# Both MLP products of a decoder block as seven block products each, with the inner layer stored in DRAM as operand pairs

## The chip, the cores and the metric

The kernel runs on one core of a Trainium2 chip. Its time is the device time of one launch, in microseconds (us); the kernel before takes 2312.52 us, the median of 3 runs (2311.11 to 2315.71). Engines: TensorE (PE; its weight loads are PEld), VectorE (DVE), ScalarE (ACT), GpSimd (POOL) and SyncE (SP), which here only issues DMAs. SBUF is the memory that all engines read; TensorE writes to the eight banks of PSUM.

## The reference

One decoder layer over 1024 tokens of width 1024, in float32. The part that the change touches is its end, the MLP:

```python
x = x + merged @ w_o                                  # "Wo": 1024 x 1024
h2 = rms_norm(x, norm_mlp_g)
x = x + jnp.square(jax.nn.relu(h2 @ w_mlp_in)) @ w_mlp_out   # 1024 x 4096, then 4096 x 1024
```

Ahead of it stand a projection, differential attention, a short convolution, attention over a memory and a gated merge of the three. They are the same in both kernels.

## The kernel before

All matrix products work on pairs: a float32 operand is kept as hi (a float32r rounding) and lo = raw - hi, and one product is three passes, hi*hi + hi*lo + lo*hi. A pair costs one ACT copy with rounding (L196 for weights) and one subtraction, on DVE or POOL by turns (L178).

Wo (L840 to L862) goes over three column groups of w_o (384, 384 and 256 wide) and, in each, over eight tiles of 128 tokens. In the last group `x2_norm` (L824) norms a finished token tile into `xn`, and `h2.put` (L233) transposes it on TensorE and splits it; the first four tiles are put between the passes of later Wo tiles (L848 to L851), the other four between the passes of the first MLP columns (L884 to L887).

The MLP goes over the hidden layer in 16 groups of 256 columns. `up` (L865) makes 128 hidden columns for 512 tokens in 24 matmuls of 512 columns, then relu (ACT, L876), square (POOL, L877), and the split into uh and ul (ACT L878, DVE L879). The second product takes the group's 256 rows of w_mlp_out for all 8 token tiles and both 512-column halves, 6 matmuls each, and DVE adds the two PSUM banks of a tile to `acc` in SBUF (L908, 1024 wide). In the last group each half is added and stored at once (L914).

Each product of the MLP is so 1536 matmuls of 512 columns: 3072 in all.

TensorE runs its instructions in the order of the program (`T.pin`, L80), loads on SP likewise (L92). The order on DVE, ACT and POOL is set by a scheduler. Each engine works through its own queue in order and waits for semaphores.

Of the kernel before, what the change touches and what calls it, by code (L numbers as in the profile page):

```python
# [15 lines left out]
F32 = mybir.dt.float32  # L16
# [8 lines left out]
P = 128  # L25
# [30 lines left out]
def tile_hybrid_block(ctx: ExitStack, tc: tile.TileContext, x, mem, norm_mix_g, norm_mem_g, w_in, b_gate,  # L56
# [9 lines left out]
    class InOrder:  # L66
        """Instructions of one queue, kept in the order of the program."""
# [10 lines left out]
    class T:  # L78
        """The tensor engine."""
# [26 lines left out]
    pool = ctx.enter_context(tc.tile_pool(name="pool", bufs=1))  # L106
    psum = ctx.enter_context(tc.tile_pool(name="psum", bufs=2, space=PSUM))
# [72 lines left out]
    def load_w(src, n, kind, eng=None):  # L180
        """src [K, n] -> (his, los), over k tiles, of [128, n] float32r APs."""
# [21 lines left out]
    def mm3_steps(ps, lhs, rhs):  # L203
        """ps = sum over k of lhs[k]^T rhs[k]; lhs, rhs = (his, los). Yields after each pass."""
# [10 lines left out]
    class ByTok:  # L215
        """[1024 channels, 1024 tokens] pair written by token tiles: slots of 2 k tiles and 512 tokens."""
# [16 lines left out]
        def put(self, t, xn, parts=(0, 4)):  # L233
            """Transposes the rows xn [128 tok, 1024] into place."""
# [11 lines left out]
    class ByChan:  # L246
        """The same written by channel tiles: a slot for each k tile."""
# [15 lines left out]
    def norm_rows(xt, g_row, step=D):  # L263
        """rms-normed rows [128, 1024] times the gain, in place."""
# [18 lines left out]
    # ================= memory: keys and values =================  # L283
# [30 lines left out]
    def normed(ps):  # L314
        """ps [128, 256] rms-normed along its rows, in SBUF."""
# [26 lines left out]
    def put_x(t):  # L342
        """The next half of a token tile."""
# [44 lines left out]
    # ================= memory attention =================  # L388
# [3 lines left out]
    def q_proj(i):  # L392
        """Yields after each pass; the last leaves the normed rows."""
# [7 lines left out]
    def run(gen, n=None):  # L401
        """Advances gen by n steps (all of them without n)."""
# [53 lines left out]
    # ================= filler work beside the attention: convolution, gate logits =================  # L456
# [39 lines left out]
    def fill_steps():  # L496
# [5 lines left out]
        # the last two units by halves, so that the first half of hT is free early  # L502
# [13 lines left out]
    # ================= output projections of the branches, gated merge =================  # L516
# [6 lines left out]
    def prep(b):  # L523
        """Loads of a branch: first weights, the branch's rows."""
# [56 lines left out]
    # ================= differential attention =================  # L581
# [19 lines left out]
    def qkv(s):  # L601
        """Projections of token tile t for head h, norms of q and k."""
# [24 lines left out]
    def qk_transposes(s):  # L627
# [7 lines left out]
        # q of either component on both halves of the partitions; k's hi, and on the other half what it leaves  # L635
# [14 lines left out]
    def scores(s):  # L650
        """Scores, softmax numerators; e0 becomes e0 - e1 * lam * s0 / s1."""
# [13 lines left out]
        for c in range(2):  # L665
            sc = scs[c]
            # sc = -(sc + mask), negm = -max(sc + mask)
# [30 lines left out]
    def values(s):  # L698
        """o = a v / s0, rms-normed along the head's 128 columns."""
# [88 lines left out]
    for s in range(ns):  # L788
        # steps of the filler: before the scores, beside the softmax, before the values, behind them
# [28 lines left out]
    # ================= output projection, residual =================  # L818
    acc = [slot(f"acc{t}", F32) for t in range(NT)]
    h2 = ByTok("h2")  # L820
# [3 lines left out]
    def x2_norm(t):  # L824
# [3 lines left out]
        xn = xns[t] = rowt("xn")  # L828
        V.scalar_tensor_tensor(out=xn, in0=acc[t], scalar=r, in1=g2_row, op0=ALU.mult, op1=ALU.mult)

    us = {}
    w1 = {}
    NB = DFF // 256

    def load_w1(j):
        if j < 2 * NB:
            w1[j] = load_w(w_mlp_in[:, j * P:(j + 1) * P], P, "wh")

    w = ready.pop("wo")
    for j, (c0, n, _) in enumerate(wos):  # L840
        for t in range(NT):
# [5 lines left out]
            steps = mm3_steps(ps, mT.tok(t), w)  # L847
            if j == 2 and 2 <= t < 6:  # L848
                for k0 in (0, 4):
                    run(steps, 10)  # L850
                    h2.put(t - 2, xns[t - 2], (k0,))  # L851
            run(steps)
# [3 lines left out]
            if j == 2:  # L856
                if t == 0:
                    h2.alloc(0)
                if t == 6:
                    load_w1(0)  # L860
                x2_norm(t)
        w = wn  # L862

    # ================= MLP =================
    def up(j, hf):  # L865
        run(up_steps(j, hf))

    def up_steps(j, hf):
        """relu(h2 @ w1)^2 for 128 columns of the hidden layer, half of the tokens."""
        if hf == 0:  # L870
            us[j] = [slot(f"u{c}") for c in "hl"]
        sl = slice(hf * 512, (hf + 1) * 512)
        ps = ps_mm()
        yield from mm3_steps(ps, w1[j], h2.half(hf))
        r = small("osl", (P, 512))
        A.activation(r, ps, AF.Relu)  # L876
        G.tensor_tensor(out=r, in0=r, in1=r, op=ALU.mult)  # L877
        A.copy(out=us[j][0][:, sl], in_=r)  # L878
        V.tensor_tensor(out=us[j][1][:, sl], in0=r, in1=f(us[j][0])[:, sl], op=ALU.subtract)  # L879

    load_w1(1)
    h2.alloc(1, "m")
    steps = chain(up_steps(0, 0), up_steps(1, 0))
    for t in range(4, NT):  # L884
        for k0 in (0, 4):
            run(steps, 6)
            h2.put(t, xns[t], (k0,))  # L887
    run(steps)
    up(0, 1)
    load_w1(2)  # L890
    w2 = load_w(w_mlp_out[0:256, :], S, "fw")
# [56 lines left out]
```

## Time and profile before

| | us |
|---|---|
| median of the runs | 2312.52 |
| span of the profiled execution | 2311.5 |
| Wo, first to last matmul | 1511.4 to 1604.5 |
| MLP, last matmul ends | 2308.2 |
| PE busy over the span | 2273.5 (98%) |
| DVE, ACT, POOL busy | 1105.3, 889.2, 645.0 |

Shares of busy time are means over very different stages. In the MLP TensorE is never idle, while DVE is busy for 231.5 of 600 us and POOL for 126.4 (the stretch from 1650 to 2250 us).

### The profile page before, as it was taken

The numbers are of one execution on the slowest core, as the hardware profiler recorded it, in microseconds if no ns is written. First come the engines' busy times: TensorE is split into PE (matmuls) and PEld (weight loads), VectorE is DVE, ScalarE is ACT, GpSimd is POOL, SyncE is SP. The second block draws the span as 40 slices with busy tenths as digits, with TensorE's granted clock in tenths as the row PEclk, the third lists the DMA queues.
The fourth block names the chain that finished last, engine by engine and source line by source line (L and its number), as shares of the span: only waits on it lengthen the run. The fifth ranks groups of instructions, "written<-read, shape, count | busy, mean of one in ns | idle before, by whom it ended". The sixth has DMA issues, their size and how long they took to land.

```text
span 2311.5 us, 31433 instructions
## 1 busy us (share of the span) xinstructions
PE 2273.5 (98%) x11814; PEld 1974.5 (85%) x11814; DVE 1105.3 (48%) x2164; ACT 889.2 (38%) x2244; POOL 645.0 (28%) x837
## 2 busy tenths in 40 slices
PE   6999999999999999999999999999999999999999
PEld 6999888888888888888887888899888888888887
DVE  6655455555555555555556234325334434434334
ACT  5644454454545454544446233323221221221220
POOL 4422223232323232232324133312221221221211
PEclk9999999999999999999999999999999999999999
DMA  6312111121212121221214444323111111111111
GB/s 196 128 64 65 46 62 58 48 80 48 71 42 83 42 80 31 69 60 40 80 51 151 137 134 158 120 80 94 54 46 46 55 46 46 55 46 46 53 30 73
DMA packets 185992, 168.39 MB, mean 73 GB/s; under 512 B 14064, under 2 KB 163824, under 8 KB 185840
## 3 DMA queue, kind: packets, MB, share of 16 engines
q1 hardware_dynamic: 166512, 136.86, 19.1%
q10 hardware_dynamic: 19328, 29.52, 3.6%
q8 instruction: 93, 1.52, 0.3%
q14 instruction: 59, 0.48, 0.1%
HBM read 137.00 MB, written 29.36 MB: 72 GB/s over the span
## 4 chain that ended last, share of the span: by engine, by line
PE 91%; DVE 3%; ACT 2%; DMA 2%; issue 1%; POOL 0%; SPq 0%; ACTq 0%; DVEq 0%; POOLq 0%
PE ps_mm L84 60%; PE ps_sc L84 26%; PE ps_tr L88 3%; PE ps_tr L84 3%; DVE ql L646 1%; ACT qh L641 1%; DMA rawh<-in_w_in_dram 1%; ACT whi L196 0%; DMA raw<-in_w_mem_kv_dram 0%; DMA memt<-in_mem_dram 0%; POOL wlo L178 0%; DVE e L680 0%; DVE whl L178 0%; DVE wlo L178 0%; DMA raw<-in_w_in_dram 0%
## 5 line engine op out<-in xcount | busy, mean ns | idle before, releaser
L84 PE MATMUL ps_mm<-hT,whi 128*128 128x512 f32 x1536 | 491.0, 401 | 0.9 <-DVE vst L616 0.9
L178 POOL TENSOR_TENSOR wlo<-raw,whi 128x384 fp32r<-128x384 f32 (+3 forms) x192 | 233.7, 1220 | 648.4 <-ACT whi L196 645.1
L196 ACT CAST whi<-raw 128x256 fp32r<-128x256 f32 (+3 forms) x392 | 206.7, 561 | 458.2 <-PE ps_sc L84 309.7
L84 PEld LDWEIGHTS ps_mm<-hT,whi 128*128 128x128 f32 x1536 | 279.4, 189 | 52.5 <-DVE vst L616 3.9
L84 PE MATMUL ps_mm<-h,whi 128*128 128x512 f32 x1024 | 316.0, 390 | 0.0
L84 PE MATMUL ps_mm<-hT,wlo 128*128 128x512 f32 x768 | 302.2, 394 | 0.0
L84 PE MATMUL ps_mm<-whh,hT 128*128 128x384 f32 x1024 | 276.4, 340 | 1.9 <-DVE inner L465 1.9
L178 DVE TENSOR_TENSOR wlo<-raw,whi 128x256 fp32r<-128x256 f32 (+2 forms) x200 | 172.1, 863 | 162.2 <-ACT whi L196 161.4
L908 DVE TENSOR_TENSOR acc<-ps_sc,acc 128x1024 f32<-128x1024 f32 x120 | 147.0, 1225 | 197.9 <-PE ps_sc L84 197.9
L84 PEld LDWEIGHTS ps_mm<-h,whi 128*128 128x128 f32 x1024 | 191.6, 188 | 39.2
L84 PE MATMUL ps_mm<-h,wlo 128*128 128x512 f32 x512 | 199.3, 389 | 0.0
L84 PE MATMUL ps_sc<-wlo,uh 128*128 128x512 f32 x496 | 192.7, 389 | 0.0
L84 PE MATMUL ps_sc<-whi,ul 128*128 128x512 f32 x496 | 192.7, 389 | 0.0
L84 PE MATMUL ps_sc<-whi,uh 128*128 128x512 f32 x496 | 192.7, 389 | 0.0
L84 PEld LDWEIGHTS ps_mm<-whh,hT 128*128 128x128 f32 x1024 | 186.3, 188 | 7.2 <-DVE inner L465 3.7
L84 PE MATMUL ps_mm<-whl,hT 128*128 128x384 f32 x512 | 171.4, 335 | 0.0
L84 PEld LDWEIGHTS ps_mm<-hT,wlo 128*128 128x128 f32 x768 | 144.7, 188 | 27.5
L618 POOL TENSOR_TENSOR sq<-qk 128x256 f32<-128x256 f32 x64 | 43.2, 675 | 392.1 <-ACT qk L613 391.8
L168 POOL TENSOR_TENSOR r<-r,mhalf 128x1 f32<-128x1 f32 (+1 forms) x186 | 132.0, 710 | 15.3
L167 POOL TENSOR_SCALAR r<-ss 128x1 f32<-128x1 f32 (+1 forms) x186 | 36.9, 198 | 321.8 <-ACT ps_tr L712 127.7
L84 PE MATMUL ps_mm<-x,whi 128*128 128x512 f32 x384 | 118.9, 391 | 0.0
L84 PE MATMUL ps_sc<-x,whi 128*128 128x512 f32 x384 | 118.3, 389 | 0.0
(176 smaller groups left out, 4083.0 us busy)
## 6 DMA issues: line engine op xcount, KB each, us to landing
raw<-in_w_in_dram SPq DMA_DIRECT2D x56, 512.0 KB, 3.8
raw<-in_w_mlp_in_dram SPq DMA_DIRECT2D x32, 512.0 KB, 4.1
raw<-in_w_mlp_out_dram SPq DMA_DIRECT2D x32, 512.0 KB, 3.7
rawh<-in_w_in_dram SPq DMA_DIRECT2D x64, 192.0 KB, 2.8
z_dram<-z ACTq DMA_DIRECT2D x24, 512.0 KB, 3.0
gt<-z_dram SPq DMA_DIRECT2D x24, 512.0 KB, 3.7
raw<-in_w_mem_kv_dram SPq DMA_DIRECT2D x16, 512.0 KB, 5.8
xt<-in_x_dram SPq DMA_DIRECT2D x8, 512.0 KB, 4.1
```

What stands on the lines that cost most here:

```text
L84: return cls.pin(nc.tensor.matmul(*a, **kw))
L88: return cls.pin(nc.tensor.transpose(*a, **kw))
L167: G.tensor_scalar(r, ss, 1.0 / n, EPS, op0=ALU.mult, op1=ALU.add)
L168: G.tensor_tensor(out=r, in0=r, in1=mhalf[:, 0:width], op=ALU.pow)
L178: eng.tensor_tensor(out=lo, in0=raw, in1=f(hi), op=ALU.subtract)
L196: A.copy(out=hi[:, a:b, :], in_=raw[:, k0 + a:k0 + b, :])
L618: G.tensor_tensor(out=sq, in0=qk, in1=qk, op=ALU.mult)
L641: A.activation(qh[z, c, :], tp[a, 0, :], AF.Copy, scale=gcol[a, :])
L646: V.scalar_tensor_tensor(out=ql[z, c, :], in0=tp[a, 0, :], scalar=gcol[a, :], in1=f(qh)[a, c, :], op0=ALU.mult, op1=ALU.subtract)
L908: V.tensor_tensor(out=acc[t], in0=ps, in1=acc[t], op=ALU.add)
```

## The change

Both MLP products are cut into 2x2 blocks, and the four blocks of the result are made from seven block products in place of eight. The operands of the seven are sums and differences of blocks: with a for the blocks of the weights, s1 = a21 + a22, s2 = s1 - a11, a11 - a21 and a12 - s2, and the same forms for the other operand (t1 to t4). The sum is made in float32, and each operand is then split into a pair. `ORDER` names the seven.

- **Wo** is left as it is, but `xn` of each token tile and the residual `acc` go to DRAM (`xn_dram` on ACT's queue, `x2_dram` on SP's queue), and all pools are closed behind it.
- **X operands**: `x_pair` loads two token tiles, transposes them, and makes the seven pairs X for these tokens, 256 of the 1024 tokens at a time (128 of each half): 9 ACT instructions, 8 on DVE and 3 on POOL.
- **First product**: 16 units of 2x128 hidden columns; a unit is seven products of 12 matmuls (K = 512, 512 columns). `Weights.make` makes the seven weight pairs of a unit, up to 5 products ahead. Unit 0 is run twice, with 256 columns each, the second time for the tokens of the last two `x_pair`s. Three partial sums of a unit stay in PSUM and are copied by ACT (`snap`) while later products go on adding to the same bank. The four results are made on DVE (`out`), their three differences and t4 on POOL and DVE by turns (`later`), and all seven are split (`emit`) and stored to `u_dram`, 512 KB each, on SP's queue.
- **Second product**: 8 chunks of 512 hidden rows; a chunk is seven products of 4 token tiles, each 6 matmuls of 512 columns. Its operands come back from `u_dram`, 1 MB each, four products ahead; the seven pairs of w_mlp_out are made three products ahead. After each product DVE adds each PSUM bank to `acc2` (512 wide). The residual is added from `x2_dram` by POOL in chunks 2 and 3.

The core of the diff:

```diff
+        store(xn_dram[t], xn)
+        nc.sync.dma_start(x2_dram[t], acc[t])
...
+    old.close()
+    ORDER = (1, 2, 6, 5, 7, 4, 3)
+    def split(hi, lo, raw, eng):
+        A.copy(out=hi, in_=raw)
+        sub(eng, lo, raw, f(hi))
...
+            if i == 6:
+                self.s1, self.s2 = self.temp(), self.temp()
+                add(self.sums(), self.s1, a21, a22)
+                sub(self.sums(), self.s2, self.s1, a11)
+                raw = self.s2
...
+            hi, lo = self.op[i] = self.pair()
+            split(hi, lo, raw, self.los())
...
+    usums, ulos, tsums = Turns([V]), Turns([G, V, G]), Turns([G, V])
...
+            if src is None:
+                A.activation(t, ps, AF.Relu)
+                V.tensor_tensor(out=t, in0=t, in1=t, op=ALU.mult)
+            else:
+                add(V, t, ps, src)
+                V.scalar_tensor_tensor(out=t, in0=t, scalar=0.0, in1=t, op0=ALU.max, op1=ALU.mult)
...
+            split(hl[:, 0, :], hl[:, 1, :], raw, ulos())
+            nc.sync.dma_start(u_dram[u // 2, k - 1, :, :, u % 2, cs], f(hl))
...
+        load_unit1(0)
+        rows = {p: row_blocks(p) for p in range(2)}
...
+        ahead = 5
+        for n in range(ahead):
+            prep1(seq, n)
+        x_pair(0, rows[0])
+        rows[2] = row_blocks(2)
+        x_pair(1, rows[1])
...
+        for n, (u, i, c0, cn) in enumerate(seq):
+            prep1(seq, n + ahead)
...
+            product1(u, i, c0, cn)
+            run_later(1)
...
+    dsums, dlos = Turns([V]), Turns([G, G, V, G, G, V, G])
...
+        load_u(seq2, n + 4)
+        prep2(seq2, n + 3)
...
+            mm7(ps, [[uo[:, h, k, p * P:(p + 1) * P] for k in range(2)] for h in range(2)],
+                [[wt[h][:, k, :] for k in range(2)] for h in range(2)], i in (1, 2, 5))
...
+            if c == 0 and i in (1, 6, 5, 4):
+                A.copy(out=a, in_=ps)
+            else:
+                add(V, a, ps, a)
```

V is DVE, G is POOL, A is ACT; `Turns([G, V, G])` hands the calls to the engines in that rotation. `mm7` issues the three passes for each K tile.

The first place is DVE at the end of Wo. Before: `xn` is the normed tile, `h2` its transposed pair, `wlo` a weight's lo part.

```order
L829 SCALAR_TENSOR_TENSOR xn_16431<-acc6_15550,r_16428,g_row_15553 128x1024
L854 TENSOR_TENSOR acc7_15551<-ps_mm_16435,qd_16433 128x256
L178 TENSOR_TENSOR wlo_16476<-raw_16469,whi_16475 128x384
L178 TENSOR_TENSOR wlo_16660<-raw_16657,whi_16659 128x384
L826 TENSOR_REDUCE ss_16462<-sums2_15552 128x1
L244 TENSOR_TENSOR h2110_16487<-ps_tr_16500,h2010_16483 128x2x128
```

In the changed kernel `w1` is a weight's pair and `st` one of its sums, `w1raw` the loaded block, `tp` a transposed tile in PSUM, `x11` the lo part of X1:

```order
L836 SCALAR_TENSOR_TENSOR xn_16389<-acc7_15553,r_16386,g_row_15555 128x1024
L877 TENSOR_TENSOR w1_16441<-w1raw_16416,w1_16441 128x512
L880 TENSOR_TENSOR st_16444<-w1raw_16416 128x512
L877 TENSOR_TENSOR st_16445<-st_16444,w1raw_16416 128x512
L877 TENSOR_TENSOR st_16454<-w1raw_16416 128x512
L877 TENSOR_TENSOR st_16585<-w1raw_16416,st_16445 128x512
L877 TENSOR_TENSOR x11_16403<-tp_16459,x10_16402 128x4x128
```

The weights' and the tokens' preparation that stood between Wo's tiles now stands behind the last of them, in one piece.

The second place is POOL in the middle of the MLP. Before, in one group of the hidden layer (`osl` is the squared relu):

```order
L877 TENSOR_TENSOR osl_19714<-osl_19714 128x512
L178 TENSOR_TENSOR wlo_19832<-raw_19825,whi_19831 128x384
L877 TENSOR_TENSOR osl_19744<-osl_19744 128x512
L877 TENSOR_TENSOR osl_19790<-osl_19790 128x512
L178 TENSOR_TENSOR wlo_20028<-raw_20025,whi_20027 128x384
L178 TENSOR_TENSOR wlo_20036<-raw_20025,whi_20035 128x256
```

Now, in the first product, `hl` is a split result on its way to `u_dram`, `t1` and `t2` are differences of results (`b`):

```order
L877 TENSOR_TENSOR hl_17490<-b11_17487,hl_17490 128x512
L877 TENSOR_TENSOR t1_17512<-b12_17509,b11_17314 128x512
L877 TENSOR_TENSOR t2_17559<-b22_17413,t1_17512 128x512
L877 TENSOR_TENSOR w1_17569<-st_17566,w1_17569 128x512
L877 TENSOR_TENSOR hl_17537<-t3_17535,hl_17537 128x512
L877 TENSOR_TENSOR hl_17561<-t2_17559,hl_17561 128x512
```

And DVE in the same unit (`Z` is a PSUM bank, `u2` and `u3` are ACT's copies of one):

```order
L880 TENSOR_TENSOR b12_17509<-Z_17373,u2_17360 128x512
L877 TENSOR_TENSOR w1_17543<-st_17541,w1_17543 128x512
L1053 SCALAR_TENSOR_TENSOR b12_17509<-b12_17509 128x512
L877 TENSOR_TENSOR st_17714<-w1raw_17295,st_17566 128x512
L877 TENSOR_TENSOR t3_17535<-b22_17413,b12_17509 128x512
L877 TENSOR_TENSOR hl_17514<-t1_17512,hl_17514 128x512
```

Every POOL row, and every DVE row but the first, has both inputs in SBUF.

## Rows read from the trace of the kernel before

**Rows 1.** The page: busy us of the engines, TensorE's granted clock by slices.

```profile
PE 2273.5 (98%) x11814; PEld 1974.5 (85%) x11814; DVE 1105.3 (48%) x2164; ACT 889.2 (38%) x2244; POOL 645.0 (28%) x837
PEclk9999999999999999999999999999999999999999
```

**Rows 2.** Chain of waits from Wo to the end: start us, us, what.

```profile
1511.39 73.54 PE ps_mm L84 x442
1584.93 0.44 PE ps_tr L88 x4
1585.36 1.19 PE ps_mm L84 x10
...
1598.23 6.25 PE ps_mm L84 x52
...
1644.41 21.76 PE ps_sc L84 x96
...
2307.44 0.73 PE ps_mm L84 x6
...
2308.20 0.42 DVE acc L914
```

**Rows 3.** Stretches: busy us of PE, PEld, DVE, ACT, POOL, PE clock, DMA share, GB/s.

```profile
0.00:30.00 30.00, 15.92 (x100) 15.15 (x101) 15.45 (x26) 15.90 (x37) 13.36 (x29) 1.00 0.87 241
39.40:42.80 3.40, 3.40 (x18) 3.40 (x19) 1.15 (x3) 1.12 (x4) 0.74 (x2) 0.54 0.35 95
1650.00:2250.00 600.00, 600.00 (x2649) 496.99 (x2648) 231.54 (x218) 126.77 (x215) 126.40 (x108) 1.00 0.15 47
```

**Rows 4.** Instructions of single tiles: count, ns shortest/median/longest.

```profile
L571 POOL TENSOR_TENSOR merged<-merged,gt x32: 1278/1293/1675, 1347.3 to 1512.2; 128x512 f32<-128x512 f32 x32
L879 DVE TENSOR_TENSOR ul<-osl,uh x64: 681/692/1091, 1617.3 to 2289.7; 128x512 fp32r<-128x512 f32 x64
L914 DVE TENSOR_TENSOR acc<-ps_mm,acc x9: 425/691/692, 2287.7 to 2308.2; 128x512 f32<-128x512 f32 x8, 128x256 f32<-128x256 f32 x1
L908 DVE TENSOR_TENSOR acc<-ps_sc,acc x120: 1224/1225/1225, 1647.2 to 2275.5; 128x1024 f32<-128x1024 f32 x120
```

**Rows 5.** Timeline from 1242 us, POOL, then DVE: start us, us, instruction.

```profile
1247.46 3.57 POOL L178 TENSOR_TENSOR x<-rawx,x 128x512 fp32r<-128x512 f32 x2 [1.63 <-ACT x L538]
1248.07 3.50 DVE L178 TENSOR_TENSOR x<-rawx,x 128x512 fp32r<-128x512 f32 x2
```

**Rows 6.** Groups by form: busy us, mean ns of one, idle before.

```profile
L196 ACT CAST whi<-raw 128x512 fp32r<-128x512 f32 x120 | 68.6, 620 | 30.4 <-PE ps_mm L84 12.7 <-issue 10.7 <-DMA raw<-in_w_mem_kv_dram 4.8
...
L178 POOL TENSOR_TENSOR wlo<-raw,whi 128x512 fp32r<-128x512 f32 x60 | 82.2, 1370 | 105.6 <-ACT whi L196 105.4
...
L178 POOL TENSOR_TENSOR wlo<-raw,whi 128x1024 fp32r<-128x1024 f32 x16 | 40.5, 2532 | 301.3 <-ACT whi L196 301.3
...
L178 DVE TENSOR_TENSOR wlo<-raw,whi 128x1024 fp32r<-128x1024 f32 x16 | 39.4, 2460 | 0.5 <-ACT whi L196 0.5
```

**Rows 7.** The page: DMA queues (MB, share of 16 engines), issues (us to landing).

```profile
q1 hardware_dynamic: 166512, 136.86, 19.1%
q10 hardware_dynamic: 19328, 29.52, 3.6%
...
raw<-in_w_mlp_in_dram SPq DMA_DIRECT2D x32, 512.0 KB, 4.1
...
z_dram<-z ACTq DMA_DIRECT2D x24, 512.0 KB, 3.0
```

**Rows 8.** PE before that clock drop: start us, us, [idle before <-releaser].

```profile
36.96 0.39 PE L84 MATMUL ps_sc<-wlo,memTh 128*128 128x256 f32 x1 [2.11 <-DVE wlo L178]
39.22 0.39 PE L84 MATMUL ps_sc<-wlo,memTh 128*128 128x256 f32 x1 [1.64 <-POOL wlo L178]
40.76 0.41 PE L84 MATMUL ps_sc<-whi,memTl 128*128 128x256 f32 x1
40.97 0.41 PE L84 MATMUL ps_sc<-whi,memTh 128*128 128x256 f32 x1
```

More of the change, by code (lines that the diff above doesn't have):

```diff
@@ L816, in tile_hybrid_block @@
     run(stream)
+    x2_dram = dram.tile([NT, P, S], F32, name="x2_dram")
+    xn_dram = dram.tile([NT, P, S], F32, name="xn_dram")
     acc = [slot(f"acc{t}", F32) for t in range(NT)]
-    h2 = ByTok("h2")
     sums2 = const.tile([P, NT, 3], F32, name="sums2")
@@ L846, in tile_hybrid_block @@
             ps = ps_mm(n)
[L847 to L852, printed above, removed]
+            mm3(ps, mT.tok(t), w)
             a = acc[t][:, c0:c0 + n]
@@ L856, in tile_hybrid_block @@
             if j == 2:
[L857 to L860, printed above, removed]
                 x2_norm(t)
         w = wn
[L865 to L879, printed above, removed]
@@ new lines, in mm7 @@
+    def mm7(ps, lhs, rhs, start):
+        n = len(lhs[0])
+        for k in range(n):
+            for i, (a, b) in enumerate(((0, 0), (0, 1), (1, 0))):
+                T.matmul(ps, lhsT=lhs[a][k], rhs=rhs[b][k], start=start and k == 0 and i == 0,
+                         stop=k == n - 1 and i == 2, skip_group_check=True)
+    xp = ctx.enter_context(tc.tile_pool(name="xp", bufs=1, reuse_waits="tile"))
+    bp = ctx.enter_context(tc.tile_pool(name="bp", bufs=1, space=PSUM, reuse_waits="tile"))
@@ new lines, in bank, with slot8, raw8, half_row @@
+    def bank(name):
+        return bp.tile([P, 512], F32, tag="b", bufs=8, name=name)
+    def slot8(name, shape, dtype=F32R):
+        return xp.tile([P, *shape], dtype, tag="x", bufs=14, name=name)
+    def raw8(name):
+        return xp.tile([P, 2048], F32, tag="wraw", bufs=2, name=name)
+    X = {i: [slot8(f"x{i}{c}", (4, 512)) for c in range(2)] for i in ORDER}
+    def half_row(name):
+        return xp.tile([P, 512], F32, tag="stg", bufs=8, name=name)
+    def row_blocks(p):
+        rows = {}
+        for t in range(2):
+            for kh in range(2):
+                rows[kh, t] = half_row("xr")
+                load(rows[kh, t], xn_dram[2 * p + t][:, kh * 512:(kh + 1) * 512])
+        return rows
@@ new lines, in x_pair, with tps, put @@
+    def x_pair(p, rows):
+        cols = slice(p * P, (p + 1) * P)
+        def tps(kh, th):
+            tp = bank("tp")
+            for j in range(4):
+                T.transpose(tp[:, j * P:(j + 1) * P], rows[kh, th][:, j * P:(j + 1) * P], ident)
+            return tp
+        def put(i, src, eng):
+            hi, lo = (X[i][c][:, :, cols] for c in range(2))
+            split(hi, lo, src.rearrange("p (k n) -> p k n", k=4), eng)
+        b11 = tps(0, 0)
+        put(1, b11, V)
+        r11 = half_row("r11")
+        A.copy(out=r11, in_=b11)
+        b12 = tps(0, 1)
+        t1 = half_row("t1")
+        sub(V, t1, b12, r11)
+        r12 = half_row("r12")
+        A.copy(out=r12, in_=b12)
+        put(5, t1, G)
+        b22 = tps(1, 1)
+        t2 = half_row("t2")
+        sub(V, t2, b22, t1)
+        put(6, t2, G)
+        t3 = half_row("t3")
+        sub(V, t3, b22, r12)
+        put(7, t3, G)
+        put(3, b22, V)
+        b21 = tps(1, 0)
+        put(2, b21, V)
+        t4 = half_row("t4")
+        sub(V, t4, b21, t2)
+        put(4, t4, V)
@@ new lines, in tile_hybrid_block, with load2, begin2, temp @@
+    body()
+    w2v = w_mlp_out.rearrange("(c g u p) n -> p c g u n", c=NC, g=2, u=2, p=P)
+    dsums, dlos = Turns([V]), Turns([G, G, V, G, G, V, G])
+    W2, raw2, U = {}, {}, {}
+    def load2(c):
+        raw2[c] = [raw8("w2raw").rearrange("p (u n) -> p u n", u=2) for _ in range(2)]
+        for g in range(2):
+            load(raw2[c][g], w2v[:, c, g])
+    def begin2(c):
+        r = raw2.pop(c)
+        a11, a12, a21, a22 = (r[g][:, :, n0:n0 + 512] for n0 in (0, 512) for g in range(2))
+        def temp():
+            return xp.tile([P, 2, 512], F32, tag="hl", bufs=6, name="st2")
+        def pair():
+            t = slot8("w2", (2, 2, 512))
+            return t[:, 0], t[:, 1]
+        W2[c] = Weights(a11, a12, a21, a22, temp, pair, dsums, dlos)
@@ new lines, in prep2, with load_u @@
+    def prep2(seq, n):
+        if n < len(seq):
+            c, i = seq[n]
+            if i == 1:
+                begin2(c)
+            W2[c].make(i)
+            if i == 3 and c + 1 < NC:
+                load2(c + 1)
+    def load_u(seq, n):
+        if n < len(seq):
+            c, i = seq[n]
+            t = U[c, i] = slot8("uop", (2, 2, 512))
+            (store if n < 4 else load)(f(t), u_dram[c, i - 1])
+    seq2 = [(c, i) for c in range(NC) for i in ORDER]
+    acc2 = []
+    with tc.high_priority(offset=300):
+        load2(0)
+        for n in range(3):
+            prep2(seq2, n)
+            load_u(seq2, n)
+            if n == 1:
+                for p in range(NP):
+                    pair = slot8(f"acc{p}", (2, S), F32)
+                    acc2 += [pair[:, 0], pair[:, 1]]
```

187 lines of the change are left out of this document (141 added, 46 removed).

## The prediction, made before the changed kernel had run

> **What bounds the kernel now.** First the busy line and the clock line of the page [rows 1]: TensorE is busy 98% of the span, and its clock is full in all forty slices, so before the change a matmul less is time less. Second the chain of waits [rows 2]. From 1511.4 us to the last matmul it is TensorE all the way: 96 matmuls of 512 columns take 21.76 us, 0.2267 each, ten of 256 columns 1.19 us, 0.119 each. 3072 x 0.2267 = 696.3 us is the MLP. From Wo's last matmul (1598.23 + 6.25 = 1604.5) to the last one (2308.2) are 703.7 us, which leaves 7.4: 3.5 for eight groups of transposes of 0.44 and 3.9 lost. Third the stretch from 1650 to 2250 us [rows 3]: TensorE 600 of 600, DVE 231.5, POOL 126.4. Here the other engines have room, and the change spends it.
>
> **What is removed.** The first product becomes 15 units of 84 matmuls of 512 columns, and one run as 168 of 256; the second is 8 chunks of 168 of 512. (1260 + 1344) x 0.2267 + 168 x 0.119 = 610.3 us against 696.3: 86.0 saved. A unit is 19.0 us of TensorE, a chunk 38.1. The rest is what this uncovers.
>
> **Prices.** POOL takes 1.29 us for a two-input operation of 512 columns, DVE 0.69, from SBUF or with one input in PSUM [rows 4]. But both have a long side, 1675 and 1091 ns, and where both engines work on SBUF without a pause [rows 5] two on POOL take 3.57 us and two on DVE, at the same time, 3.50. So a pair costs about 1.75 us; one after the other they would take 1.98, side by side 1.29. A DVE operation with PSUM input is never slowed: 1224 to 1225 ns over 120 [rows 4]. ACT's cast of 512 takes 0.62 [rows 6]. I take 1.75 for each pair of a POOL and a two-SBUF-input DVE operation, bounds 1.29 and 1.98.
>
> The Trainium skill (page "SBUF — State Buffer", section "Who interferes with whom") calls the port pair that the two share an exclusive lock, held for whole instructions. The trace agrees in direction: both stretch. By the lock a pair would cost the full 1.98; the row has 1.75.
>
> **Start-up of the first product.** Before, weights and tokens are prepared between Wo's tiles. Now this stands behind Wo's last tile. Without the transposes Wo ends at 1604.5 - 3.5 = 1601.0. Behind it, on SP's queue, come the last residual's store, two weight loads of 512 KB and the row loads. A store of 512 KB takes 3.0 us to land, a load 4.1 [rows 7]; norm, store and reload in series put the first work on tokens at about +9. From there to the last X operand DVE has 28 operations of 512 with PSUM input (19.3 us), 14 with two SBUF inputs (9.7) and 8 of 256 columns, 0.425 each [rows 4], 3.4: together 32.4, plus about 6 behind POOL's 17 operations (half of them meeting, 0.7 each). 1601 + 9 + 32.4 + 6 = about 1649 for X and with it the start of the main stage. Bounds: 1640 (no collision, loads early) and 1664 (every collision and a late store). TensorE has only 27 us of work in these 48, so it waits in pieces of microseconds. The clock answers to that: after waits of 2.11 and 1.64 us [rows 8] it stood at 0.54 from 39.4 to 42.8 us [rows 3], with 256-column matmuls 0.21 us apart in place of 0.12. If all 27 us ran so, they would be 27 x 0.21 / 0.119 = 48, the same as DVE's time; so I cost the clock at nothing here.
>
> **First product.** From 1649 to the last weight pair of the first product POOL has 157 operations of 512, 13 of 256 and one of 1024, as 165.5 of 512; DVE 204 of 512 and 11 of 256 with two SBUF inputs, as 209.5, and 41 of 512 from PSUM. TensorE has 15 units, 285.6 us. Each engine alone fits under that: POOL 165.5 x 1.29 = 213.5, DVE 209.5 x 0.69 + 42.5 x 0.69 = 174, ACT 265 x 0.62 = 164. Together on the port: 165.5 pairs x 1.75 = 289.6, and the other 44 of DVE x 0.69 = 30.4, which makes 320 us, 34 over TensorE. DVE's PSUM operations go beside POOL's own work, and weight pairs are made up to five products ahead, so most waits are absorbed; I add 6 for what is not, 326 (21.7 a unit). Bounds: 285.6 (TensorE) and 213.5 + 144.6 = 358 (every operation at its full duration, none beside another).
>
> Cost at nothing: the stores of results and the loads of weights, 4.72 MB a unit. The queues moved 136.86 MB in 19.1% of the span, 310 GB/s when at work [rows 7], by which a unit needs 15.2 us, under 21.7. The first 30 us had 241 GB/s at 0.87 share [rows 3]; at 241 it is 19.6 us. ACT's snaps run under the products that follow, as long as the bank's next use is a product later.
>
> **From the first to the second product.** TensorE's last unit ends 2.7 us behind its last weight pair (one product, 12 x 0.2267). Then the second product needs its own weights, prepared in the posts' way on the same two engines (21 DVE operations stand behind the first product's last weight pair), and operands that are stored and loaded back: 3.0 + 4.1 us in series [rows 7]. The first chunk's operands were stored long before; the last units' belong to chunk 8 alone. I take 8 us, between 3 and 12.
>
> **Second product.** 1344 x 0.2267 = 304.7. In a chunk of 38.1 us DVE has 28 adds of one bank (0.69 each, 19.3) and 6 operations of 1024 with two SBUF inputs, between 1.22 (the bank form [rows 4]) and 2.46 (beside POOL [rows 6]), so 26.6 to 34.1; POOL 5 of 2.53, 12.7, and 8 residual adds in two of the chunks (10.3 more). DVE is close but under. Loads are 9.4 MB a chunk, 30 us at 310 GB/s, 39 at 241: close too. I take 6 us of stalls, between 2 and 10. The end is as before, with an add of 512 in place of 256: before 2311.5 - 2308.2 = 3.3 us, now 3.3 + 0.27, taken as 3.8 for the wider store.
>
> **Sum.** 1649 + 326 + 2.7 + 8 + 304.7 + 6 + 3.8 = 2300.2 us of span. The median lies 1.0 above the profiled execution's 2311.5, so 2301 us.
>
> **Rivals.**
> (B) Collisions are hidden and TensorE bounds the first product. For it: each engine alone fits with 70 us to spare, and the shortest cases (1278 and 681 ns) show pairs that miss each other. Against it: [rows 5]. X at 1649, unit 0's last product about 3 us behind it: 1652 + 285.6 + 3 + 304.7 + 2 + 3.8 + 1.0 = 2252.
> (C) Slower: POOL's and DVE's operations exclude each other in full in the first product, and TensorE waits for weight pairs in every unit. Price 358 us in place of 326; it decides over faster or slower once this stage passes 337 us, 22.5 a unit (2301 + 11 = 2312). 1649 + 358 + 2.7 + 12 + 304.7 + 10 + 3.8 + 1.0 = 2341. For it: every POOL row of the first product reads two tiles in SBUF, and the waits are short and many, which is what dropped the clock in [rows 8]. Against it: 1.75, not 1.98, where the two met without pause. The lock rule of the Trainium skill, named above, would end here.
> (D) DMA bounds the first product. If stores and loads mixed on one queue fall to 196 GB/s, as an estimate a fifth under the 241 of [rows 3], a unit takes 24.1 us: 1649 + 361 + 2.7 + 12 + 304.7 + 10 + 3.8 + 1.0 = 2344. Against it: 310 GB/s [rows 7].
> That the change doesn't do what it says I rule out: the program holds 2772 matmuls in place of 3072.
>
> **How the numbers follow.** The forecast (the port binds part of the time) 0.60, with a range of its own from 2278 (main stage 310, transition and stalls at their low ends) to 2325 (X at 1655, main stage 340, the rest a little over); B 0.16; C 0.18; D 0.06. A measurement of this kernel tells no change from 0.2%, 2307.9 to 2317.1 us. Of the forecast's 0.60, 0.41 is below that, 0.11 in it and 0.08 above. Faster 0.41 + 0.16 = 0.57, same 0.11, slower 0.08 + 0.18 + 0.06 = 0.32. The range takes in most of B and of C: 2256 to 2340.
>
> **What the profile after would show.** A unit of the first product 21 to 22.5 us apart, not 19.0; POOL's operation of 512 at a mean of 1.5 or more and DVE's with two SBUF inputs above 0.85, against 1.29 and 0.69; TensorE's waits there released by the weight pairs' lo parts on POOL or DVE; 20 to 25 us of idle TensorE between 1601 and 1652; a chunk of the second product within 1.5 us of 38.1. Wrong would be: units at 19.1 (B); units at 24 with waits on the stores' buffers or on weight loads (D); or means at the low end with TensorE waiting all the same, in which case the order of the queues binds and not the port. If TensorE's clock stands well under 1.0 in the first product, waits cost twice and C is nearer.

## The result, and the profile after

The changed kernel takes 2341.4 us, the median of 4 runs (2341.14 to 2342.15), against 2314.11 for the kernel before on the same chip: 1.0119 times as long, 95% interval 1.0105 to 1.0133. It is slower, by 1.2%; the forecast was 2301 and faster, and the time lies 1.4 us above the range.

First the page of the changed kernel (busy us, then tenths in 40 slices and the granted clock), to be held against [rows 1]:

```profile
PE 2219.3 (95%) x11508; PEld 1920.4 (82%) x11508; DVE 1369.4 (59%) x2449; ACT 975.6 (42%) x2363; POOL 917.2 (39%) x965
...
PE   6999999999999999999999999996899898799999
...
DVE  5755455555555555555555324316788888566665
...
POOL 4422232232322232323224133303687778445322
PEclk9999999999999999999999999998999999899999
```

TensorE is busy for 54 us less than before and yet the span is 28 longer. In the first product (the 29th to the 34th slice) DVE is at 7 to 8 tenths and POOL at 6 to 8; behind it both have less to do. TensorE has slices of 8 there and one of 7 at the second product's first chunk, and its clock is no longer full everywhere.

Then the stretches, cut where the first matmul of the next stage starts: start-up (Wo's last matmul to unit 0's last), the 15 units of the first product, chunk 0 of the second, its chunks 1 to 7. The columns are those of [rows 3], the bounds cut to about 0.1 us.

```profile
1600.20:1666.30 66.10, 35.79 (x235) 33.61 (x234) 48.20 (x67) 32.33 (x67) 36.70 (x32) 0.79 0.58 186
1666.30:1997.40 331.10, 301.52 (x1263) 241.67 (x1262) 280.70 (x259) 145.89 (x268) 260.06 (x169) 0.97 0.63 215
1997.40:2050.50 53.10, 40.24 (x170) 32.82 (x169) 29.28 (x28) 19.32 (x29) 22.23 (x11) 0.87 0.80 307
2050.50:2335.90 285.40, 273.05 (x1177) 221.98 (x1175) 189.22 (x233) 48.35 (x46) 108.80 (x49) 0.99 0.63 234
```

At full speed the matmuls of these stretches need 27, 285.6, 38.1 and 266.6 us. So 39 us are lost in the start-up, 45.5 in the first product, 15.0 in chunk 0 and 18.8 in the rest: 118 us against the 86 saved. (Before, 3.9 us were lost, and the transposes, now among the 27 us, took 3.5.) A unit takes 331.1 / 15 = 22.07 us.

What TensorE waited for, after Wo (releaser: us in total, times, longest). Some of the first and of the small rows stand in the start-up; in the first product the copies cost 29.4 us.

```profile
PE X L89 <- ACT u L1043: 36.3, 21, 4.4
PE tp L93 <- DMA xr<-xn_dram: 13.7, 2, 12.8
PE X L89 <- DMA uop<-u_dram: 12.9, 1, 12.9
PE Y L89 <- DVE x L877: 5.9, 1, 5.9
PE X L89 <- DVE acc L880: 5.5, 2, 3.5
PE X L89 <- issue: 3.6, 4, 1.1
PE X L89 <- ACT w L883: 2.9, 2, 1.6
```

The largest is ACT's copy of a partial sum (`u`), which must have been taken from bank X before the next product adds to it. That copy takes 0.58 us. Why it is late is seen at 1740 us, in the timelines of POOL, DVE, ACT and TensorE, one fence each (start us, us, instruction, [idle before and releaser]):

```profile
1736.89 1.73 POOL L877 TENSOR_TENSOR hl<-b,hl 128x512 fp32r<-128x512 f32 x1
1739.32 1.61 POOL L877 TENSOR_TENSOR t<-b,b 128x512 f32<-128x512 f32 x1 [0.69 <-DVE b L1053]
1741.01 1.61 POOL L877 TENSOR_TENSOR t<-b,t 128x512 f32<-128x512 f32 x1
```

```profile
1735.72 1.76 DVE L877 TENSOR_TENSOR w<-st,w 128x512 fp32r<-128x512 f32 x1 [0.61 <-ACT w L883]
1737.41 1.77 DVE L1053 SCALAR_TENSOR_TENSOR b<-b 128x512 f32<-128x512 f32 x1
```

```profile
1736.08 0.62 ACT L883 CAST w<-st 128x512 fp32r<-128x512 f32 x1
1740.96 1.17 ACT L883 CAST hl<-t 128x512 fp32r<-128x512 f32 x2 [4.27 <-POOL t L877]
1742.65 0.62 ACT L883 CAST hl<-t 128x512 fp32r<-128x512 f32 x1 [0.51 <-POOL t L877]
1743.17 0.61 ACT L883 CAST w<-st 128x512 fp32r<-128x512 f32 x1
1743.69 0.58 ACT L1043 COPY u<-X 128x512 f32<-128x512 f32 x1
```

```profile
1736.30 5.68 PE L89 MATMUL X<-x,w 128*128 128x512 f32 x24
1744.32 4.58 PE L89 MATMUL X<-x,w 128*128 128x512 f32 x12 [2.34 <-ACT u L1043]
1748.70 1.61 PE L89 MATMUL Y<-x,w 128*128 128x512 f32 x6
```

ACT is idle for 4.27 us at the head of its queue, on a cast whose input POOL has not made; the copy for TensorE stands four instructions behind it. POOL's and DVE's operations in these rows take 1.6 to 1.77 us each. And after its 2.34 us of waiting TensorE runs the next 12 matmuls in 4.58 us in place of 2.88: the granted clock from 1740 to 1760 us is 0.91. Behind another wait of the same length it stayed full (1.00 from 1800 to 1820 us):

```profile
1811.66 3.01 PE L89 MATMUL X<-x,w 128*128 128x512 f32 x12 [2.34 <-ACT u L1043]
```

### The profile page after: what moved, and what is told of

It reads as the page before. It is cut to its first block, busy times and chain, and to the rows that moved or that the text cites. A ratio compares the mean times of both kernels' runs of the same rounds, so it can differ in the third digit from the quotient of the medians.

```text
span 2339.9 us, 32038 instructions
## 1 busy us (share of the span) xinstructions
PE 2219.3 (95%) x11508; PEld 1920.4 (82%) x11508; DVE 1369.4 (59%) x2449; ACT 975.6 (42%) x2363; POOL 917.2 (39%) x965
## 5 line engine op out<-in xcount | busy, mean ns | idle before, releaser
L184 POOL TENSOR_TENSOR wlo<-raw,whi 128x512 fp32r<-128x512 f32 (+2 forms) x128 | 146.9, 1153 | 258.2 <-ACT whi L202 254.2
L89 PE MATMUL X<-x,w 128*128 128x512 f32 (+1 forms) x816 | 197.4, 397 | 37.5 <-ACT u L1043 36.3
L89 PEld LDWEIGHTS X<-x,w 128*128 128x128 f32 x816 | 152.9, 198 | 76.9 <-ACT u L1043 46.1
L89 PE MATMUL X<-w,uop 128*128 128x512 f32 x768 | 186.5, 399 | 25.2 <-DMA uop<-u_dram 12.9
L89 PEld LDWEIGHTS X<-w,uop 128*128 128x128 f32 x768 | 146.9, 193 | 61.1 <-issue 18.4
L877 POOL TENSOR_TENSOR w<-st,w 128x512 fp32r<-128x512 f32 (+1 forms) x67 | 125.1, 1872 | 145.3 <-ACT w L883 145.3
L202 ACT CAST whi<-raw 128x512 fp32r<-128x512 f32 (+2 forms) x264 | 129.1, 532 | 88.7 <-PE ps_sc L89 36.5
L184 DVE TENSOR_TENSOR wlo<-raw,whi 128x512 fp32r<-128x512 f32 (+2 forms) x136 | 105.9, 783 | 64.0 <-ACT whi L202 63.2
L89 PE MATMUL Z<-w,uop 128*128 128x512 f32 x576 | 134.5, 389 | 0.0
L89 PEld LDWEIGHTS Z<-w,uop 128*128 128x128 f32 x576 | 108.1, 188 | 22.4
```

Of the source, the lines that this page charges most:

```text
L89: return cls.pin(nc.tensor.matmul(*a, **kw))
L184: eng.tensor_tensor(out=lo, in0=raw, in1=f(hi), op=ALU.subtract)
L202: A.copy(out=hi[:, a:b, :], in_=raw[:, k0 + a:k0 + b, :])
L877: eng.tensor_tensor(out=out, in0=a, in1=b, op=ALU.subtract)
```

## The experiments

Two theories stood for the largest loss. PORT: POOL and DVE's two-input operations on SBUF hold each other up, so that shared work costs 1.75 us a pair of operations. LOAD: DVE, 281 of 331 us busy, simply has too much to do. They differ in what happens when POOL's work is given to DVE. The "posts" are what DVE and POOL do behind the products: the lo parts of weights and results, and the differences of results. The lengths in the table are those of the four stretches above.

| kernel | median | start-up | first product | chunk 0 | chunks 1-7 |
|---|---|---|---|---|---|
| changed kernel | 2341.4 | 66.1 | 331.1 | 53.1 | 285.4 |
| p1pool | 2368.0 | 67.4 | 357.2 | 51.7 | 286.0 |
| p1dve | 2290.9 | 63.1 | 286.6 | 50.1 | 285.9 |
| p2dve | 2339.3 | 66.2 | 332.2 | 52.0 | 281.9 |
| trans | 2335.6 | 66.0 | 339.7 | 38.1 | 288.4 |
| warm | 2336.0 | 64.4 | 331.2 | 53.0 | 280.0 |
| late (on p1dve) | 2290.4 | 64.3 | 287.0 | 48.7 | 284.2 |
| rows1st (on p1dve) | 2291.9 | 66.3 | 286.8 | 49.2 | 281.9 |
| tie1 (on p1dve) | 2289.1 | 61.5 | 286.6 | 50.0 | 285.9 |
| tie2 (on p1dve) | 2273.2 | 62.0 | 286.7 | 50.1 | 268.2 |
| p1trans = p1dve + trans | 2285.6 | 62.6 | 291.6 | 38.1 | 288.7 |
| best1 = p1trans + tie1 + tie2 | 2268.0 | 61.6 | 292.9 | 38.1 | 268.2 |
| best2 = best1 + p2dve | 2265.8 | 61.5 | 292.2 | 38.2 | 266.9 |

The medians below the first are from three groups of runs; the kernel before was at 2313.1 to 2315.1 in them. The lengths are from one profiled run each, and the last column moves by up to 6 us between kernels with the same code there (280.0 to 286.0).

**p1dve: the first product's posts on DVE.**

```diff
-    usums, ulos, tsums = Turns([V]), Turns([G, V, G]), Turns([G, V])
+    usums, ulos, tsums = Turns([V]), Turns([V]), Turns([V])
```

> All lo parts and differences of the first product on DVE, none on POOL (165 operations moved; nothing else). Theory PORT (POOL and DVE exclude each other on SBUF, so a shared pair costs 1.75 us where DVE alone does its half in 0.69): DVE needs about 375 x 0.69 + 43 x 0.69 = 288 us for the 15 units, TensorE 285.6; DVE's mean for 512 columns falls back to 0.69, a unit from 22.1 to 19.2-20.2 us, the median from 2341 to 2300-2312. Rival LOAD (DVE is the bound by its own work; it is busy 281 of the 331 us already, and POOL takes work off it): 281 + 158 x 0.69 = 390 us, a unit about 25-26 us, the median near 2395.

Measured: 2290.9 us, 0.9906 of before (0.9891 to 0.9921), 50 us below the changed kernel. The first product falls to 286.6 us, TensorE's own time; the start-up, in which unit 0's posts stand, and chunk 0 fall by 3.0 each. Below are the stretch (columns as above), then groups of the first product: three of DVE's and one of POOL's in the changed kernel, and DVE's three in p1dve (count, busy us, mean ns of one, idle before):

```profile
1664.40:1951.00 286.60, 285.92 (x1262) 236.44 (x1261) 263.36 (x427) 151.07 (x268) 4.80 (x2) 1.00 0.74 250
```

```profile
L1053 DVE SCALAR_TENSOR_TENSOR b<-b 128x512 f32<-128x512 f32 x44 | 52.9, 1203 | 0.5
L877 DVE TENSOR_TENSOR hl<-t,hl 128x512 fp32r<-128x512 f32 x19 | 30.3, 1594 | 15.0 <-ACT hl L883 14.4
...
L880 DVE TENSOR_TENSOR b<-Z,u 128x512 f32<-128x512 f32 x29 | 19.7, 679 | 0.3 <-PE Z L89 0.3
```

```profile
L877 POOL TENSOR_TENSOR w<-st,w 128x512 fp32r<-128x512 f32 x38 | 59.6, 1574 | 12.1 <-ACT w L883 12.1
```

```profile
L877 DVE TENSOR_TENSOR hl<-t,hl 128x512 fp32r<-128x512 f32 x56 | 37.1, 684 | 0.0
...
L1053 DVE SCALAR_TENSOR_TENSOR b<-b 128x512 f32<-128x512 f32 x44 | 30.2, 686 | 0.1
L880 DVE TENSOR_TENSOR b<-Z,u 128x512 f32<-128x512 f32 x29 | 20.0, 691 | 14.5 <-PE Z L89 10.0 <-ACT u L1043 4.5
```

DVE carries out 427 operations in 263.4 us where it needed 280.7 for 259. With POOL at work its operations of 512 columns with two SBUF inputs averaged 1.26 us (groups from 0.69 to 1.76), alone 0.68 to 0.73; the one with an input in PSUM (`b<-Z,u`) is the same in both. LOAD is out. The clock is back at 1.00, with less than 1 us of waiting left. The run takes away three things at once: the meeting on SBUF, POOL's own slower operations (1.29 us against 0.69), and the waiting of one engine for the other. The stretched operations show the first; no run kept POOL and moved ACT's copies ahead of its casts, so how much the order alone would have given back is open.

**p1pool: the lo parts all on POOL.**

```diff
-    usums, ulos, tsums = Turns([V]), Turns([G, V, G]), Turns([G, V])
+    usums, ulos, tsums = Turns([V]), Turns([G]), Turns([G, V])
```

> The other way: all lo parts of the first product on POOL (about five more operations a unit there and five fewer on DVE; the differences stay by turns). Theory PORT: a unit has 16 POOL and 10 two-SBUF DVE operations, 10 pairs x 1.75 + 6 x 1.29 = 25.2 us, so a unit takes 25 us or a little over where the changed kernel has 22.1, the median near 2341 + 15 x 3.2 = 2389. Rival LOAD (what counts is DVE's work, which falls by a third): a unit 19.5-21, median 2300-2325.

Measured: 2368.0, 1.0227 of before (1.0213 to 1.0241), 23.8 us a unit. The direction is PORT's; the size is short of its 25.2, and the median of its 2389. The stretch shows another bound reached: POOL is busy all of it.

```profile
1669.30:2026.50 357.20, 311.70 (x1262) 250.00 (x1261) 243.57 (x191) 147.21 (x265) 357.20 (x237) 0.93 0.57 199
```

**trans: other buffers for the second product's sums.**

```diff
-            return xp.tile([P, 2, 512], F32, tag="hl", bufs=6, name="st2")
+            return xp.tile([P, 2, 512], F32, tag="wop", bufs=7, name="st2")
```

> The sums of the second product's weights take their buffers from the first product's weight pairs (free early) and not from the split results (free when stored); the order moves DVE's sums, ACT's casts and the third and fourth operand load ahead of the last results' splits. Theory QUEUE (the 12.9 us wait at the second product's third block is made of the sums' buffers and of the load standing behind ACT's last five casts): the wait falls to 0-5 us, with the slow clock behind it; median 8 to 14 lower. Rival LANDING (the operand's way through DRAM sets it: stores and loads at a DMA share near 1): the wait moves by less than 3 us, median within 3.

The wait it aims at, in the changed kernel: the third product's operand is loaded by ACT's queue, and stands there behind a cast of a sum. The sum takes its buffer from the split results, and DVE makes it behind the last of them (timelines of ACT with its queue of DMAs, then of TensorE).

```profile
2005.27 0.62 ACT L883 CAST hl<-t 128x512 fp32r<-128x512 f32 x1 [1.22 <-DVE t L877]
2010.42 1.05 ACT L883 CAST w<-st 128x1024 fp32r<-128x1024 f32 x1 [4.53 <-DVE st L877]
2010.43 1.27 ACTq L101 DMA_DIRECT2D uop<-u_dram  x2
```

```profile
2021.26 7.63 PE L89 MATMUL X<-w,uop 128*128 128x512 f32 x24 [12.86 <-DMA uop<-u_dram]
2028.73 5.60 PE L89 MATMUL Z<-w,uop 128*128 128x512 f32 x24
```

Measured: chunk 0 at 38.1 us, all 15 us gone; QUEUE holds for the wait. But the median fell by only 5.8 (2335.6), short of QUEUE's 8 to 14, because the first product became 8.6 longer: the sums now stand in its last unit, among POOL's operations, and take up to 3.38 us each. **p1trans** puts the two together:

> The first product's lo parts and differences on DVE, and the second product's sums in the weight pairs' buffers. The first alone gave 2290.9, its first product 286.6 us (TensorE 285.6) and chunk 0 of the second 50.1; with the other alone, chunk 0 fell from 53.1 to 38.1 but the first product, still with POOL, rose from 331 to 340. Theory PORT (the rise was the sums' collisions with POOL at the end of the first product): here it does not come back, or as DVE's own 0.69-1.22 an operation, below 4 us; median 2277-2283. Rival LOAD (DVE, 263 of 287 us busy, has no room for the sums): the first product rises by 8 or more again, median 2286-2291.

Measured: 2285.6 (0.9869, 0.9855 to 0.9884), the first product 291.6. The rise shrank from 8.6 to 5.0, between the two ranges (below 4, 8 or more). So 3.6 of it went with POOL; that DVE's full queue makes the rest is likely and not shown.

**p2dve: the second product's lo parts on DVE.**

```diff
-    dsums, dlos = Turns([V]), Turns([G, G, V, G, G, V, G])
+    dsums, dlos = Turns([V]), Turns([V])
```

> All lo parts of the second product's weights on DVE, none on POOL (POOL keeps the residual adds). Theory PORT: the waits at the fourth product on bank X of each chunk (0.8 to 4.8 us) come from DVE's sums and POOL's lo parts of 1024 columns holding each other up; without POOL DVE has 28 x 0.69 + 11 x 1.22 = 32.7 of 38.1 us, the waits of chunks 1, 3, 4, 6 go, those of 2 and 5 shrink; from chunk 1 to the end 285.6 becomes 274-280 us, median 6 to 11 lower. Rival LOAD (DVE's work in a row, four sums of 1024 ahead of the adds, makes the wait): DVE has 5 x 1.22 more in each chunk, waits stay or grow, median the same or up to 6 higher.

Measured: 2339.3, chunks 1 to 7 281.9: neither theory's range, and within what the column moves by itself. The total doesn't decide. Chunk by chunk TensorE's waits show more: those of chunks 1, 3 and 4 (0.83 to 0.84 us each) are gone and those of 5 and 6 fall from 3.7 and 1.1 to 0.95 and 0.4, as PORT had it; but that of chunk 2, in which POOL has most of the residual adds, grows from 4.8 to 8.4. So POOL has a part in these waits. The wait itself pointed to the order on DVE as well: timelines of chunk 1 of the changed kernel, TensorE, then DVE.

```profile
2072.25 5.60 PE L89 MATMUL X<-w,uop 128*128 128x512 f32 x24
2078.68 1.60 PE L89 MATMUL X<-w,uop 128*128 128x512 f32 x6 [0.84 <-issue]
```

```profile
2073.43 1.21 DVE L877 TENSOR_TENSOR st<-st,w2raw 128x1024 f32<-128x1024 f32 x1
2074.56 3.42 DVE L877 TENSOR_TENSOR st<-w2raw 128x1024 f32<-128x1024 f32 x1
2077.91 0.68 DVE L880 TENSOR_TENSOR acc<-X,acc 128x512 f32<-128x512 f32 x1
2078.51 1.21 DVE L877 TENSOR_TENSOR st<-w2raw,st 128x1024 f32<-128x1024 f32 x1
```

The next product writes to bank X once DVE has read it at 2077.91; that add stands behind sums for the next chunk, one of them stretched to 3.42 us (1.22 alone). **tie2** (on p1dve) lets each sum follow, on DVE, the last add issued before it:

```diff
+                tied(sub(self.sums(), raw, a12, self.s2))
...
-                add(V, a, ps, a)
+                last[:] = [add(V, a, ps, a)]
```

(`tied` adds an order, no wait on another engine, from `last[0]` to the instruction; all four sums are tied.)

> As the kernel with the first product's posts on DVE (2290.9), and the second product's sums of weights are held on DVE behind the adds of the product issued before them. Theory ORDER (the waits at the fourth block product on bank X, 0.8 to 4.8 us in each chunk, are for an add that stands behind three sums of 1024 columns): chunks 1 to 7, 285.9 us, become 268-276, median 2281-2287. Rival WEIGHTS (POOL's lo parts and the loads of w_mlp_out are what is late, and the sums, now later, come late themselves): 284 or more, median 2289 or more.

Measured: 2273.2, 0.9827 of before (0.9812 to 0.9842), 17.7 below p1dve; chunks 1 to 7 at 268.2, the clock 1.00, although POOL still works beside DVE there:

```profile
1998.50:2266.70 268.20, 266.82 (x1177) 220.46 (x1175) 177.31 (x235) 48.42 (x46) 102.71 (x49) 1.00 0.67 249
```

ORDER holds for the stretch; WEIGHTS falls. (The median lies below ORDER's 2281 to 2287: that range allowed 4 to 10 us, its own stretch 10 to 18.) One wait of TensorE is left in these chunks, of 1.38 us. The tie also moved the sums out of POOL's way: their means were 1.2 to 2.5 us in the changed kernel and are 1.2 to 1.4 here. So the waits were made by two things together, the order, which put the sums ahead of the add, and POOL, which made them long; taking POOL off the lo parts alone was not enough, tying the order nearly was.

**The start-up** was tried four times. **warm** fills waits with useless matmuls:

```diff
+            if (p, kh, th) == (0, 0, 0):
+                fill(tp, 50)
...
+        if u == 0 and c0 == 0 and i in (2, 5):
+            fill(ps, 16)
```

> 82 matmuls of 128 columns without use are put into TensorE's waits of the start-up: 50 ahead of the first transposes (a wait of 12.8 us), 16 ahead of the second and 16 ahead of the fourth product of unit 0. Theory CLOCK (the start-up's miss is in good part the clock, 0.66 to 0.84 there, which falls after waits): with the clock near 1.0 the way from Wo's end to unit 0's last matmul falls from 65.9 to 57-61 us, median 5 to 9 lower. Rival CHAIN (DVE's and ACT's work on the tokens sets the time, TensorE at half clock keeps up): 64-68 us, median within 3 of 2341, the clock higher all the same.

```profile
1598.50:1662.80 64.30, 51.60 (x398) 49.56 (x397) 48.95 (x66) 31.50 (x66) 36.18 (x31) 0.92 0.58 191
```

The clock rose from 0.79 to 0.92 and the stretch fell by 1.7 us: CHAIN, by its length. The median, 2336.0, is 5.4 lower, outside CHAIN's 3; in the profiled run most of the difference stands in chunks 1 to 7, which the edit doesn't touch.

**late** loads unit 1's weights behind the token rows, **rows1st** the first token rows ahead of unit 0's weights, and **tie1** holds unit 1's sums behind the last token operand (all on p1dve):

```diff
-                if u + 1 < NU:
+                if 0 < u < NU - 1:
                     load_unit1(u + 1)
...
                 x_pair(3, rows[3])
+                load_unit1(1)
```

```diff
-        load_unit1(0)
         rows = {p: row_blocks(p) for p in range(2)}
+        load_unit1(0)
```

```diff
-        put(4, t4, V)
+        ins = put(4, t4, V)
+        if p == NP - 1:
+            last[:] = [ins]
```

> As the kernel with the first product's posts on DVE, and unit 1's weights loaded behind all token rows, so that their four sums on DVE (about 4 us with their wait for the load) no longer stand ahead of the tokens' operands. Theory ORDER (the start-up is a chain through DVE's and ACT's queues): from Wo's last matmul to unit 0's last 63.1 becomes 57-60 us, median 3 to 6 below 2290.9. Rival DMA (the first rows, 13 us behind Wo, and the rows of the other pairs set it): 62-64 us, median within 2.

> As the kernel with the first product's posts on DVE, and the token rows of the first two pairs loaded ahead of unit 0's weights. Theory DMA (the first transpose waits 12.8 to 13.2 us for its rows, behind 1 MB of weights): the wait falls to 8-10 us, the start-up by 2 to 4, median 2287-2289. Rival SWAP (the weights are then what is late, the same bytes in another order): start-up 62-65 us, median within 2 of 2290.9.

> As the kernel with the first product's posts on DVE (2290.9), and unit 1's sums of weights are held on DVE behind the last token operand (a tie in the order only; the load stays where it was). Moving the load alone left the start-up at 64.3 us, because the sums still stood among the token operands and waited 3.8 us for the load. Theory ORDER (DVE's queue, with work nobody needs yet at its head, sets the start-up): from Wo's last matmul to unit 0's last 63.1 becomes 56-60 us, median 2284-2288. Rival ROWS (the token rows' way through DRAM and the chain on ACT and DVE set it): 62-64 us, median within 2 of 2290.9.

Measured: 64.3, 66.3 and 61.5 us, medians within 2 of 2290.9. In rows1st the first wait fell from 13.2 to 9.0 us, as DMA said, and came back later: SWAP, though 66.3 is above its 62 to 65. In late the sums stayed among the token operands and DVE waited 3.79 us for the moved load. tie1 lies between its theories, and p1trans and tie2, without the tie, have 62.6 and 62.0. None of the four shortened the start-up by 2 us or more against kernels without it. The table shows one edit that did, though it aimed elsewhere: without any of the four the start-up is 66.0 to 67.4 us with POOL at unit 0's posts (changed kernel, p1pool, p2dve, trans) and 62.0 to 63.1 with them on DVE (p1dve, tie2, p1trans). What sets these 62 us is left open; the first rows come 12 to 14 us behind Wo in every run but rows1st (9.0).

**best1, best2: what helped, together.**

> All four: posts on DVE, the second product's sums in the weight pairs' buffers, both ties. By ORDER and PORT: start-up 57-60, first product 287-290, chunk 0 38.1, chunks 1 to 7 268-276, the median 2256-2272. If the ties only move the waits (ROWS, WEIGHTS): 2280-2287.

> As the kernel before in this list, and the second product's lo parts on DVE too, so that POOL has only the residual adds and a few token operands. Theory PORT: what is left of collisions in chunks 1 to 7 goes, 267-272 us, the median 0 to 5 below the one with POOL. Rival LOAD (DVE has 32.7 of 38.1 us there, and the lo parts come late): chunks 1 to 7 274 or more, the median 2 or more above.

Measured: 2268.0 (0.9804 of before, 0.9790 to 0.9819) and 2265.8 (0.9793, 0.9779 to 0.9808). best1's start-up and first product miss their ranges (57 to 60 and 287 to 290) by 1.6 and 2.9 us; the rest is as expected. That best2 is 2 us lower is within what the runs of one kernel differ by, but LOAD, at 274 us or more for chunks 1 to 7, is out. Of best2, the four stretches:

```profile
1600.60:1662.10 61.50, 35.69 (x234) 33.62 (x233) 46.09 (x80) 32.45 (x67) 16.65 (x16) 0.78 0.58 187
1662.10:1954.30 292.20, 287.78 (x1262) 237.47 (x1262) 268.47 (x436) 152.95 (x270) 0.00 (x0) 0.99 0.75 254
1954.30:1992.50 38.20, 38.20 (x171) 31.61 (x170) 24.38 (x32) 17.09 (x26) 0.00 (x0) 1.00 0.98 362
1992.50:2259.40 266.90, 266.88 (x1177) 220.43 (x1175) 213.55 (x269) 48.32 (x46) 26.33 (x16) 1.00 0.66 250
```

The second product is at TensorE's time; 34 us of the start-up and 7 of the first product are what is left. The three gains, measured singly, are 50.5 (p1dve), 17.7 (tie2) and 5.3 us (p1trans); they add to 73.5, and best1 is 73.4 below the changed kernel. So the seven products do pay, by 47 us, once three things of the change are mended: which engine has the posts, where the sums have their buffers, and where they stand on DVE. What tie1 and p2dve add is within the noise.

## Why the prediction was wrong, point by point

The sum, term by term: unit 0 done at 1652, measured 1666.3 (+14.3); from there to the first product's end 325.7, measured 331.1 (+5.4); transition 8, measured 15.0 (+7.0); stalls in the rest of the second product 6, measured 18.8 (+12.8); the end 3.8, measured 4.0 (+0.2); median over span 1.0, measured 1.5 (+0.5). Together 40.2, the whole of 2341.4 - 2301.2. What failed is the pricing of the joints: start-up, transition and stalls were added up from durations and busy times, 34.1 us too low together, while what they cost is set by what stands ahead of what in a queue.

- **Matmuls saved: right.** With the waits out (best2) chunk 0 takes 38.2 us and the others 266.9, as worked out.
- **The port in the first product: right in size, in part by luck.** Pairs at 1.75 us gave 21.7 us a unit, measured 22.07. p1dve shows that POOL's part in the posts costs 44.5 us here. POOL's mean of 1.5 or more and DVE's above 0.85 came as listed, 1.58 and 1.26 us. But the sum had DVE busy for 320 us without a pause, and POOL for 290 of them. In the trace they are busy for 281 and 260 of 331; the rest is waiting. And the chain to TensorE was another than forecast: weight pairs' lo parts were to release its waits, but ACT's copies did, since ACT's queue stands at casts of results that are not made yet.
- **Stalls of the second product: the step whose mechanism failed.** "DVE is close but under" compared sums of a chunk and took 6 us; it was 18.8. The shares were under (189 us of 285); the order was not looked at. Within a chunk DVE makes the next chunk's sums ahead of an add on which the next product waits, and POOL's lo parts stretch these sums. tie2, which changes only the order, takes the price away, 285.9 to 268.2 us; p2dve shows POOL's part in chunks 1, 3 and 4. The residual adds were taken as 8 in each of two chunks; the changed kernel has 14 in chunk 2, the one with the longest waits (4.8 us). A chunk took 40.8 us on average, outside the 1.5 about 38.1 that were listed.
- **Start-up: the term of +9 and 38 us was too small, the largest miss (+14.3).** The first rows came 12.8 us behind Wo, with the DMA engines busy throughout (346 GB/s from 1600 to 1620 us): [rows 7] had the medians of transfers elsewhere, and here 1 MB of weights and the last stores were on the way with the rows. Of the other 10 us POOL at unit 0's posts made about 3 to 4, by the table. What is left is not settled; waits for DVE and ACT of 4 to 6 us stand there, which a sum of durations doesn't contain; TensorE is idle for 30 us of the stretch, where 20 to 25 were listed. "I cost the clock at nothing here" holds to about 2 us: warm put 0.13 of clock back and gained 1.7.
- **Transition: the bounds of 3 to 12 missed 15.0.** Of the 12.9 us of waiting the stores and loads in series were priced (7.1). The load's place on ACT's queue was not, nor the buffers of the sums, by which these come behind the last results. trans takes all of it out of chunk 0; 8.6 us come back in the first product, 5.0 with the posts on DVE.
- **The clock elsewhere** was left out except in a last sentence. In the first product TensorE was busy 301.5 us for 285.6 of work. About 10 of these 16 us stand in six places, where 12 matmuls took 1.7 us longer behind waits of 1.8 to 3.3 us; the rest is small change at every wait. In p1dve (first product) and tie2 (chunks 1 to 7) both went together.
- **Rival C's 2341 is no hit.** It had the first product at 358 us by full exclusion; that took 331. It reaches the time through its other terms. (Its point, and B's of 2252, lay just outside the stated range.) The side was decided by start-up, transition and stalls together (+34 us), with the port's 40 already in the forecast.
- **Rivals B and D.** B's main stage, TensorE alone, is what p1dve runs, so it was one line of the change away. D is out: the first product moved 250 GB/s in p1dve and TensorE did not wait for it; no run shows 196 GB/s, or any other rate, as a bound there.

## What to carry to other kernels

When a change makes two engines share work on SBUF, price the pair and then the single engine: here DVE alone did all of it faster than DVE and POOL together, because alone its operations took 0.69 us and so fitted (263 of 287 us). When an engine has several kinds of work in one queue, a share of busy time under 100% says nothing of the instruction another engine waits for; find that instruction in the order and read what stands ahead of it, and what that waits for. Take the costs of joints (start-up, transition, stalls within a stage) near the upper end of their bounds: here all three came out above the value taken.

## What the runs showed of the hardware

- POOL and DVE on SBUF, 512 columns each [rows 4, 5]: 0.69 us for DVE alone, up to 1.78 beside POOL (2.81 beside one of POOL's 1024 columns); POOL 1.29 alone, 1.58 on average beside DVE and mostly 1.75 where they meet, whether the pair comes once or for 331 us. A PSUM input spared DVE: 28 such operations stood beside POOL's in the first product, none over 0.69. It also holds where one SBUF tile is both inputs (`b<-b`, 686 ns alone, 1203 beside POOL). The Trainium skill (page "SBUF — State Buffer", section "Who interferes with whom") puts it as a lock between the two that a DVE operation with one SBUF input, outside its modes with two ports, doesn't meet. By that rule the adds from PSUM are spared, and the rows agree.
- After a wait of 2.34 us twelve matmuls took 4.58 us in place of 2.88; behind a wait of 0.80 (at 1766 us) 3.01. The length of a wait alone doesn't tell: behind the one of 2.34 us at 1811 us the clock stayed full.
- With TensorE busy throughout, the clock stood at 1.00 for 286.6 us (p1dve) and 266.9 us (best2).
- DMA at a share of 0.98 and 362 GB/s for 38 us (best2, chunk 0) did not hold TensorE up.
